# Output projection of a hybrid mixer: seven combined block products replaced by eight plain ones

## The chip, the cores and the metric

One core of a Trainium2 chip runs the whole kernel in one launch. The metric is the device time of one execution in microseconds (us). Engines are named as the profile names them: PE (TensorE, matmuls), DVE (VectorE), ACT (ScalarE), POOL (GpSimd), SP (SyncE, which here only issues DMAs). All values are float32; a matmul operand is cut into a high part and a low part, and a product of two operands is three matmuls (high by high, high by low, low by high).

## The reference

One decoder layer on 1024 tokens of width 1024. Only the first of its three residual steps is touched:

```
y_a = chunk_spatial_gating(gu, gv, ...)              # (1024 tokens, 512)
o   = gated_delta_rule(q, k, v, g, beta)             # state goes from chunk to chunk
y_b = rmsnorm(o, dn_onorm) * silu(gate)              # (1024 tokens, 512)
x   = x + concatenate([y_a, y_b], axis=-1) @ w_out   # the output projection
x   = x + CrossAttn(RMSNorm(x), RMSNorm(mem))        # memory cross-attention
x   = x + W2 relu(W1 RMSNorm(x))^2                   # the MLP, then a final RMSNorm
```

Activations are kept transposed: channels on the 128 partitions, tokens along the free dimension. `hf` is the half of the tokens (0: first 512, 1: second 512). `y_a` does not depend on the delta rule; `y_b` of a token half is known when the delta rule has passed its four chunks of 128 tokens.

## The kernel before, in words

**Order.** Input projection and the mixer's preparation come first, to about 373 us. Then a loop over 8 chunks of 128 tokens runs the delta rule. Each chunk has four steps (`chunk`, L1281 to L1330: the products with the state, with the inverse, with keys and with queries), and beside them four steps that invert the next chunk's 128x128 block (`inverse`, L1208 to L1241). The steps are short and each waits for the one before, so pieces of other work are put between them on PE: the generator `fill` hands out units of work, and `run_fill(n)` adds n to an account and runs one unit for every whole number in it. After each of the 70 places in the loop (4 steps of the first inversion, 8 x 4 chunk steps, 7 x 4 inversion steps, 6 calls between chunks) the account gets `FILL` = 0.43; 9 units run ahead of the loop (2 + 2 + `FILL0` = 5).

**The units.** 32 units prepare the cross-attention's keys and values from `mem` (each with 24 matmuls of 256 columns or 12 of 512). Each needs a 512 KB weight block: `load` puts it in one of four raw buffers, three blocks ahead; `split` cuts it into high (ACT, L134) and low parts (DVE, L135), two blocks ahead. The first 30 cuts rotate through three pairs of buffers, later ones through two (`wh`/`wl`, two buffers each). Then come 12 units of the output projection, each 12 matmuls of 128x128 by 128x512.

**The output projection before.** With the weight matrix and the activations in 2 x 2 blocks of 512, it is done by seven block products on sums and differences of blocks instead of eight plain ones. One block product is 4 units of 12 matmuls. Three of the seven are fill units: `out_use` with the first half of `y_a`, `out_use` with the difference of its halves (weights: sum of two blocks, formed on POOL), and `yb_use` with the first half of `y_b`. `out_use` adds its PSUM result to two tiles (L1079) and stores both in DRAM (`xA_d`). The other four products need the delta rule's second token half and stand after the loop, with everything for them: sums of activation blocks on DVE and POOL (`part`, L1359 to L1364), their cuts (L135), sums of weight blocks on POOL (`w_load`, `comb`, L424) and their cuts (`two`), and the evictions (L1458, L1467, L1478, L1487). `finish(c)` (L1337, L1340) transposes and gates a chunk's output; it cuts it at once only for the first token half.

**After the projection.** `x_done` stores the new x tile in DRAM, scales it for the attention (ACT, L952) and adds its square to a running sum (L205 to L209). `g_load` reads the attention's key products. The attention's first product (`split4`, `block_product`) begins at once.

**Who sets the order.** Inside `tc.manual_schedule(engines={PE})` matmuls run in the order written; the order of DVE, ACT, POOL and of SP's DMAs is set by the framework's planner on its own estimates. Before, that region ends with the last fill unit, ahead of the four late products. All engines run their queue in that fixed order.

Of the kernel before, what the change touches and what calls it, by code (L numbers as in the profile page):

```python
# [31 lines left out]
FILL0, FILL = 5, 0.43  # L32
# [203 lines left out]
def hybrid(ctx, tc, t, out):  # L236
# [720 lines left out]
    def fill():  # L957
# [79 lines left out]
        def ya_split(gi, hf):  # L1037

            a = YA[gi][hf]
            if hf == 1:  # L1040
                nc.gpsimd.tensor_tensor(a, a, YA[gi][0], op=ALU.subtract)
            hi = T(f"A{2 * gi + hf}", [P, 512], F32R)
            lo = T(f"A{8 + 2 * gi + hf}", [P, 512], F32R)
            e.split_copy(hi, lo, a)
            YX[gi][hf] = (hi, lo)

        x_in = deque()
        x_next = iter([(False, hf, p) for q in range(2) for hf in range(2) for p in (2 * q, 2 * q + 1)]
                      + [(True, 0, 0), (True, 0, 2)])

        def x_load():

            for sums, hf, p in x_next:
                if sums:
                    a = e.R("Z4 Z5", [P, 2, 512])
                    src = xA_d[p * P:(p + 2) * P, h512(hf)].rearrange("(b r) t -> r b t", r=P)
                else:
                    a = e.R("Y4 Y5 Y6 Y7", [P, 2, 512])
                    src = t["xT"][:, h512(hf)].rearrange("(b p r) t -> p r b t", b=2, r=P)[p]
                nc.sync.dma_start(a, src)  # L1060
                x_in.extend((a[:, b], p + b if sums else 4 * b + p, hf) for b in range(2))
                break

        def rows_of(w, p):
            return [v[:, :, (p % 2) * P:(p % 2) * P + P] for v in w]

        chain = {}

        def out_use(w, p, hf):

            if hf == 0:
                chain[p] = e.mm()
            ps = chain[p]
            wh, wl = rows_of(w, p)
            for k in range(4):
                e.mm3(ps[:], wh[:, k], wl[:, k], *YX[k][hf], hf == 0 and k == 0, k == 3, more=hf == 1)
            for b in range(2):
                a, m, _ = x_in.popleft()
                nc.vector.tensor_tensor(a, ps[:], a, op=ALU.add)  # L1079
                nc.scalar.dma_start(blk(xA_d, m, hf), a)  # L1080
            x_load()

        def yb_use(w, p):

            ps = e.mm()
            wh, wl = rows_of(w, p)
            for k in range(4):
                e.mm3(ps[:], wh[:, k], wl[:, k], YH[k // 2][:, k % 2], YL[k // 2][:, k % 2],
                      k == 0, k == 3)
            a, m, hf = x_in.popleft()  # L1090
            nc.vector.tensor_tensor(a, ps[:], a, op=ALU.add)
            x_done(m, hf, a, "xr0 xr1")
            x_load()
# [10 lines left out]
        ya[first_out + 1] = [(gi, 1) for gi in range(4)]  # L1104
        wo = t["w_out"]
        for q in range(2):
            for hf, src in enumerate((wo[0, q], (wo[0, 2 + q], wo[1, 2 + q]))):
                for p in (2 * q, 2 * q + 1):
                    add(src if p % 2 == 0 else None, [P, 4, 256],
                        lambda w, p=p, hf=hf: out_use(w, p, hf))  # L1110
        for q in range(2):
            for p in (2 * q, 2 * q + 1):
                add(wo[1, q] if p % 2 == 0 else None, [P, 4, 256], lambda w, p=p: yb_use(w, p))
# [5 lines left out]
        def load():  # L1119
            if need:  # L1120
                src, shape, _ = work[need.pop(0)]
                parts = []
                for d in src if isinstance(src, tuple) else (src,):
                    n = e.ring.get("raws", 0)
                    e.ring["raws"] = n + 1
                    tag = RAWS[n % len(RAWS)]
                    parts.append(T(tag, shape, F32, RAW if tag == "raw" else 1))
                    nc.sync.dma_start(parts[-1], d)
                if len(parts) == 2:
                    nc.gpsimd.tensor_tensor(parts[0], parts[0], parts[1], op=ALU.add)  # L1130
                raws_.append((parts[0], shape))
# [29 lines left out]

    fills = fill()
    debt = [0.0]

    def run_fill(n):
        debt[0] += n
        while debt[0] >= 1:
            debt[0] -= 1
            if next(fills, 1) == 1:
                debt[0] = -1e9  # L1170
# [163 lines left out]
    def finish(c, hf, sl, o, gc):  # L1334
# [3 lines left out]
        for a in range(2):  # L1338
            y = YR[hf][a][:, :, sl]
            nc.vector.tensor_tensor(y, ps[:, 256 * a:256 * a + 256].rearrange("p (h t) -> p h t", t=P),  # L1340
                                    gc[:, 2 * a:2 * a + 2], op=ALU.mult)
            if hf == 0:
                e.split_copy(YH[a][:, :, sl], YL[a][:, :, sl], y)

    def slot4(*tags):
        return [(t_[:, 0], t_[:, 1]) for t_ in (T(n, [P, 2, 512], F32R) for n in tags)]

    def split_part(q, src, sl):
        for (hi, lo), x in zip(ops_[q], src):
            e.split_copy(hi[:, sl], lo[:, sl], x[:, sl])  # L1350

    def part(sl):

        if "B22" not in ops_:
            ops_["B22"] = slot4("Z0", "Z1", "Z2", "Z3")
            ops_["T2"] = slot4("Y4", "Y5", "Y6", "Y7")
        split_part("B22", B22, sl)
        for x, y in zip(T1, B22):
            nc.vector.tensor_tensor(x[:, sl], y[:, sl], x[:, sl], op=ALU.subtract)  # L1359
        split_part("T2", T1, sl)  # L1360
        for x, y in zip(T1, B11):
            nc.gpsimd.tensor_tensor(y[:, sl], x[:, sl], y[:, sl], op=ALU.subtract)
        for x, y in zip(T1, B21):
            nc.gpsimd.tensor_tensor(y[:, sl], y[:, sl], x[:, sl], op=ALU.subtract)  # L1364


    def w_load(p):

        q, sl = p // 2, slice((p % 2) * P, (p % 2) * P + P)
        slots = ((0, 1, 2, 3, 4), (5, 7, 8, 10, 13))[p % 2]  # L1370
        a11, a12, a21, a22, s1 = (T(f"B{b}", [P, 4, P]) for b in slots)
        for a, (kb, cb) in ((a21, (0, 2 + q)), (a22, (1, 2 + q)), (a11, (0, q)), (a12, (1, q))):
            nc.sync.dma_start(a, t["w_out"][kb, cb, :, :, sl])
        comb([s1], [a21], [a22], ALU.add)
        comb([a21], [a11], [a21])
        comb([a11], [s1], [a11])
        comb([a12], [a12], [a11])
        return a12, a11, a21, a22

    def two(a, b):  # L1380

        w = [T(t_, [P, KT, P], F32R, 2) for t_ in ("wh", "wl")]
        for i, src in enumerate((a, b)):
            e.split_copy(w[0][:, 4 * i:4 * i + 4], w[1][:, 4 * i:4 * i + 4], src)
        return w
# [16 lines left out]
    YR = [[T(f"E{2 * hf + a}", [P, 2, 512]) for a in range(2)] for hf in range(2)]  # L1402
    YH, YL = ([T(f"E{4 + 2 * b + a}", [P, 2, 512], F32R) for a in range(2)] for b in range(2))
    B21, B22 = (both_halves(y) for y in YR)
    ops_ = {}
    steps(inverse(0))
    for c in range(NC):
        extra = [inverse(c + 1)] if c + 1 < NC else []
        if c == NC - 1:
            raw = w_load(0)  # L1410
# [7 lines left out]
    B11, T1 = ([y[hf] for y in YA] for hf in range(2))  # L1418
    run_fill(FILL)
    part(slice(0, 384))  # L1420
    run_fill(2)
    OUT[NC - 1]()
    part(slice(384, 512))
    run_fill(1e6)
    wa = two(*raw[:2])
    region.__exit__(None, None, None)

# [10 lines left out]
    g_load(0, 0)  # L1438

    def out_product(ps, w, b, q, start):  # L1440
        for k in range(4):
            e.mm3(ps[:], w[0][:, 4 * b + k], w[1][:, 4 * b + k], *ops_[q][k], start and k == 0, k == 3,
                  more=not start)

    def x_part(m, hf):

        a = e.R("xr0 xr1 F0 F1", [P, 512])
        nc.sync.dma_start(a, blk(xA_d, m, hf))
        return a

    for p in range(4):
        s3, a22 = raw[2:]
        a = x_part(p, 1)

        def s4_product():
            ps = e.mm()
            out_product(ps, wa, 0, "B22", True)
            nc.vector.tensor_tensor(a, ps[:], a, op=ALU.add)  # L1458

        if p == 0:  # L1460
            s4_product()
            wb = two(s3, a22)
        if p < 3:
            raw = w_load(p + 1)
        ps = e.mm()
        out_product(ps, wa, 1, "T2", True)
        nc.vector.tensor_tensor(a, ps[:], a, op=ALU.add)  # L1467
        if p > 0:
            s4_product()
        if p < 3:  # L1470
            wa = two(*raw[:2])
        if p == 0:
            ops_["T3"] = slot4("E4", "E5", "E6", "E7")
            split_part("T3", B11, slice(0, 512))
        x_done(p, 1, a, "F2 F3", nc.vector)
        a = x_part(4 + p, 1)
        out_product(ps, wb, 0, "T3", False)
        nc.vector.tensor_tensor(a, ps[:], a, op=ALU.add)  # L1478
        if p == 0:
            ops_["T4"] = slot4("Z4", "Z5", "Z6", "Z7")  # L1480
            split_part("T4", B21, slice(0, 512))
# [697 lines left out]
```

## Time and profile before

| | |
|---|---|
| median of 3 runs | 1471.27 us (1466.73 to 1472.91) |
| the profiled execution | 1479.01 us, its span 1477.3 us |
| PE busy | 1372.3 us (93% of the span), 6790 matmuls |
| DVE busy | 1196.2 us (81%) |
| ACT, POOL busy | 711.2 us (48%), 419.0 us (28%) |
| mean granted PE clock | 0.958 of full |

Busy shares are means over the whole span. Matmuls are pipelined, and their shown durations overlap: how fast they go is read from the distance of their starts. A wait is shown as idle time in front of an instruction, with the instruction that ended it.

### The profile page before, as it was taken

The page shows a single profiled execution, that of the slowest core. Times are in us where ns is not written, and L with a number is a line of the kernel's source. Part 1 is how long each engine was busy: PE and PEld are TensorE (multiplying, and loading weights), DVE is VectorE, ACT ScalarE, POOL GpSimd, SP SyncE. Part 2 cuts the span into 40 slices and gives each one's busy share as a digit, 9 for nine tenths or more (in the row PEclk, how much of TensorE's full clock was granted, in tenths as well). Part 3 has the DMA queues.
Part 4 walks back from the last instruction along what each step waited for, and adds up shares of the span by engine and source line. Part 5 has one row for each costly group of instructions (what it writes and reads, how often), then busy time and mean ns, then how long its engine had stood idle before and what let it go on. Part 6 is the DMA issues. An engine that isn't in the chain of part 4 may idle for free.

```text
span 1477.3 us, 19249 instructions
## 1 busy us (share of the span) xinstructions
PE 1372.3 (93%) x6790; PEld 1134.7 (77%) x6790; DVE 1196.2 (81%) x1795; ACT 711.2 (48%) x1266; POOL 419.0 (28%) x314
## 2 busy tenths in 40 slices
PE   9989989889999988889979799999998999999996
PEld 8767777668898766667758588888886788888885
DVE  8798878798577788899999976776777998787775
ACT  7453565646455436565746644344443443333432
POOL 7542545520311263773495600000000000000024
PEclk9999999989999998999989899999999999999996
DMA  5103344539988865414000144444446754534203
GB/s 202 44 29 100 101 136 118 146 119 342 298 270 249 270 235 156 158 63 149 17 29 1 43 157 150 157 157 157 156 139 232 280 186 154 171 128 143 71 1 114
DMA packets 144979, 215.27 MB, mean 146 GB/s; under 512 B 22897, under 2 KB 82289, under 8 KB 144882
## 3 DMA queue, kind: packets, MB, share of 16 engines
q1 hardware_dynamic: 92320, 156.79, 33.6%
q10 hardware_dynamic: 52562, 57.25, 11.3%
q8 instruction: 53, 0.87, 0.2%
q14 instruction: 44, 0.36, 0.1%
HBM read 145.84 MB, written 68.16 MB: 145 GB/s over the span
## 4 chain that ended last, share of the span: by engine, by line
PE 48%; DVE 20%; DMA 5%; issue 4%; ACT 3%; POOL 1%; ACTq 0%; DVEq 0%; SPq 0%; POOLq 0%
PE mm L155 10%; PE mm L156 10%; PE mm L157 9%; PE dn L155 5%; PE dn L156 5%; PE dn L157 5%; DVE Z L135 3%; DVE Y L135 3%; DVE wl L135 2%; DVE F L607 1%; DVE A L1726 1%; DVE rw L2059 1%; DMA hid_T_d<-F 1%; DMA g_d<-A 1%; ACT wh L134 1%
## 5 line engine op out<-in xcount | busy, mean ns | idle before, releaser
L2041 POOL TENSOR_TENSOR rB<-rB,fq 128x256 f32<-128x256 f32 (+1 forms) x18 | 18.9, 1050 | 596.4 <-ACT fq L2039 595.9
L155 PE MATMUL mm<-A,wh 128*128 128x512 f32 (+1 forms) x336 | 124.7, 371 | 7.8 <-ACT F L518 5.3
L157 PE MATMUL mm<-A,wl 128*128 128x512 f32 (+1 forms) x336 | 122.9, 366 | 0.0
L134 ACT CAST wh<-raw 128x512 fp32r<-128x512 f32 (+1 forms) x105 | 78.9, 767 | 71.9 <-PE dn L156 22.8
L135 DVE TENSOR_TENSOR wl<-raw,wh 128x512 fp32r<-128x512 f32 (+1 forms) x99 | 94.9, 960 | 16.7 <-ACT wh L134 16.3
L156 PE MATMUL mm<-B,wh 128*128 128x512 f32 x220 | 89.6, 407 | 0.0
L134 ACT CAST sp<-rw 128x1024 fp32r<-128x1024 f32 x36 | 37.6, 1051 | 92.5 <-issue 42.0
L155 PEld LDWEIGHTS mm<-A,wh 128*128 128x128 f32 x336 | 66.7, 199 | 18.0 <-ACT F L518 6.1
L157 PEld LDWEIGHTS mm<-A,wl 128*128 128x128 f32 x336 | 66.8, 199 | 9.2 <-DVE wl L135 0.5
L155 PE MATMUL mm<-Z,wh 128*128 128x512 f32 x130 | 53.1, 410 | 7.8 <-DVE xr L1478 4.2
L155 PE MATMUL mm<-sp,sp 128*128 128x512 f32 (+1 forms) x152 | 58.1, 385 | 2.1 <-DVE A L2085 2.1
L156 PE MATMUL mm<-sp,sp 128*128 128x512 f32 (+1 forms) x152 | 58.2, 383 | 1.6 <-DVE sp L135 1.6
L424 POOL TENSOR_TENSOR B<-B,B 128x512 f32<-128x512 f32 x32 | 47.6, 1503 | 41.6 <-DMA B<-in_w_out_dram 18.9
L157 PE MATMUL mm<-sp,sp 128*128 128x512 f32 (+1 forms) x152 | 58.1, 383 | 0.0
L1922 DVE TENSOR_TENSOR F<-raw 128x512 f32<-128x512 f32 x15 | 10.4, 691 | 58.0 <-DMA raw<-in_ffn_w_dram 58.0
L156 PE MATMUL mm<-Z,Z 128*128 128x512 f32 (+1 forms) x136 | 53.6, 394 | 2.8 <-DVE Z L135 2.7
L135 DVE TENSOR_TENSOR sp<-rw,sp 128x1024 fp32r<-128x1024 f32 x36 | 43.8, 1218 | 14.3 <-ACT sp L134 14.3
L156 PE MATMUL mm<-Z,wh 128*128 128x512 f32 x130 | 53.1, 408 | 0.3 <-DVE Z L135 0.3
L155 PE MATMUL mm<-Z,Z 128*128 128x512 f32 (+1 forms) x136 | 53.4, 393 | 0.0
L157 PE MATMUL mm<-Z,wl 128*128 128x512 f32 x130 | 53.1, 409 | 0.0
L157 PE MATMUL mm<-Z,Z 128*128 128x512 f32 (+1 forms) x136 | 53.0, 390 | 0.0
L2017 DVE TENSOR_TENSOR A<-mm,A 128x512 f32<-128x512 f32 x64 | 43.5, 685 | 9.6 <-PE mm L157 9.4
(702 smaller groups left out, 4629.4 us busy)
## 6 DMA issues: line engine op xcount, KB each, us to landing
raw<-in_ffn_w_dram SPq DMA_DIRECT2D x32, 512.0 KB, 3.7
raw<-in_w_in_dram SPq DMA_DIRECT2D x20, 512.0 KB, 3.9
rw<-hid_T_d SPq DMA_DIRECT2D x18, 512.0 KB, 3.3
hid_T_d<-F ACTq DMA_DIRECT2D x33, 256.0 KB, 2.4
rw<-hid_B_d SPq DMA_DIRECT2D x14, 512.0 KB, 3.3
Z<-in_ffn_w_dram SPq DMA_DIRECT2D x12, 512.0 KB, 4.4
rw<-in_ffn_w_dram SPq DMA_DIRECT2D x12, 512.0 KB, 4.8
hid_B_d<-F ACTq DMA_DIRECT2D x22, 256.0 KB, 2.4
```

The costliest lines, as they stand in the source:

```text
L134: nc.scalar.copy(hi, src)
L135: (lo_eng or nc.vector).tensor_tensor(lo, src, hi.bitcast(F32), op=ALU.subtract)
L155: nc.tensor.matmul(out, wh, xh, start=start, stop=False, skip_group_check=more)
L156: nc.tensor.matmul(out, wh, xl, start=False, stop=False, skip_group_check=more)
L157: nc.tensor.matmul(out, wl, xh, start=False, stop=stop, skip_group_check=more)
L424: eng.tensor_tensor(x, y, z_, op=op)
L607: nc.vector.scalar_tensor_tensor(acc, pre[:, tap:tap + 512], g_of("conv", 12 * tap + self.blk), acc, op0=ALU.mult, op1=ALU.add)
L1726: nc.vector.tensor_tensor(acc, ps[:], acc, op=ALU.add)
L1922: nc.vector.tensor_tensor(s1, a21, a22, op=ALU.add)
L2017: nc.vector.tensor_tensor(acc, ps[:], acc, op=ALU.add)
L2041: nc.gpsimd.tensor_tensor(self.sa, self.sa, self.sq, op=ALU.add)
L2059: nc.vector.scalar_tensor_tensor(ob[:, b], acc, g_of("norm_final", m), rb, op0=ALU.mult, op1=ALU.mult)
```

## The change

The output projection becomes eight plain block products, 32 units of 12 matmuls: 16 with `y_a` (both halves), 8 with the first half of `y_b`, 8 with its second half. All are units of `fill`, which has 64 units instead of 44. `FILL` goes from 0.43 to 0.56. Units 57 to 64 (second half of `y_b`) are held back until a last call; units 49 to 56 are called behind the loop, two ahead of the last `finish` and six behind it. `finish` cuts both halves of `y_b`. `part`, `w_load`, `two`, the weight sums and the whole section of four late products go. The region in which PE's order is the written one now reaches to the last unit. The attention's `g_load`s stand ahead of the last 8 units.

```
-FILL0, FILL = 5, 0.43
+FILL0, FILL = 5, 0.56
...
-            if hf == 1:
-                nc.gpsimd.tensor_tensor(a, a, YA[gi][0], op=ALU.subtract)
...
+        x_next = iter([(False, hf, c) for c in range(4) for hf in range(2)]
+                      + [(True, hf, c) for hf in range(2) for c in range(4)])
...
+        def out_use(w, b, ops_):
+            ps = e.mm()
+            wh, wl = (v[:, :, b * P:(b + 1) * P] for v in w)
             for k in range(4):
+                e.mm3(ps[:], wh[:, k], wl[:, k], *ops_(k), k == 0, k == 3)
             a, m, hf = x_in.popleft()
             nc.vector.tensor_tensor(a, ps[:], a, op=ALU.add)
+            if b == 1:
+                x_load()
+            return a, m, hf
+
+        def ya_use(w, b, hf):
+            a, m, hf = out_use(w, b, lambda k: YX[k][hf])
+            nc.scalar.dma_start(blk(xA_d, m, hf), a)
+
+        def yb_use(w, b, hf):
+            a, m, hf = out_use(w, b, lambda k: tuple(v[hf][k // 2][:, k % 2] for v in (YH, YL)))
+            x_done(m, hf, a, ("xr0 xr1", "F2 F3")[hf], (None, nc.vector)[hf])
...
+        for c in range(4):
+            for hf in range(2):
+                for b in range(2):
+                    add(wo[0, c] if hf + b == 0 else None, [P, 4, 256],
+                        lambda w, b=b, hf=hf: ya_use(w, b, hf))
+        for hf in range(2):
+            if hf == 1:
+                before.append(len(work))
+            for c in range(4):
+                for b in range(2):
+                    add(wo[1, c] if b == 0 else None, [P, 4, 256],
+                        lambda w, b=b, hf=hf: yb_use(w, b, hf))
...
+    def run_fill(n, last=False):
         debt[0] += n
+        while debt[0] >= 1 and (last or not before or ran[0] < before[0]):
             debt[0] -= 1
+            ran[0] += 1
...
         for a in range(2):
-            y = YR[hf][a][:, :, sl]
+            y = e.R("B2 B3", [P, 2, P])
             nc.vector.tensor_tensor(y, ps[:, 256 * a:256 * a + 256].rearrange("p (h t) -> p h t", t=P),
                                     gc[:, 2 * a:2 * a + 2], op=ALU.mult)
-            if hf == 0:
-                e.split_copy(YH[a][:, :, sl], YL[a][:, :, sl], y)
+            e.split_copy(YH[hf][a][:, :, sl], YL[hf][a][:, :, sl], y)
...
-    run_fill(FILL)
-    part(slice(0, 384))
     run_fill(2)
     OUT[NC - 1]()
-    part(slice(384, 512))
-    run_fill(1e6)
-    wa = two(*raw[:2])
-    region.__exit__(None, None, None)
+    run_fill(60)
...
+    for hp in range(2):
+        for kb in range(2):
+            g_load(kb, hp)
+    debt[0] = 0.0
+    run_fill(1e6, True)
+    region.__exit__(None, None, None)
```

## Rows read from the trace of the kernel before

**Rows 1.** Windows: length, busy of PE, PEld, DVE, ACT, POOL, PEclk, DMA share, GB/s.
```profile
373.40:531.10 157.70, 151.65 (x1265) 136.06 (x1265) 108.61 (x213) 73.74 (x129) 43.47 (x35) 0.96 0.89 275
531.10:622.10 91.00, 73.38 (x280) 56.21 (x279) 81.10 (x103) 46.89 (x91) 49.84 (x40) 0.89 0.51 169
622.10:660.00 37.90, 32.21 (x151) 26.30 (x150) 37.43 (x49) 22.12 (x46) 29.75 (x19) 1.00 0.16 55
373.40:499.60 126.20, 122.11 (x1060) 110.87 (x1060) 83.79 (x164) 64.06 (x112) 30.30 (x25) 0.95 0.88 270
499.60:531.10 31.50, 29.54 (x207) 25.19 (x205) 24.82 (x50) 9.68 (x18) 13.16 (x10) 1.00 0.91 298
```

**Rows 2.** Timeline of PE: start us, length us, instruction; [idle before it <-releaser].
```profile
530.27 1.06 PE L1314 MATMUL dn<-B,Z 128*128 128x128 f32 x8
531.09 0.48 PE L155 MATMUL mm<-A,wh 128*128 128x512 f32 x1
...
621.69 0.55 PE L157 MATMUL mm<-Z,wl 128*128 128x512 f32 x1
```

**Rows 3.** Timeline of PE, first and last matmul of one fill unit.
```profile
543.22 0.39 PE L155 MATMUL mm<-E,wh 128*128 128x512 f32 x1
...
545.71 0.39 PE L157 MATMUL mm<-E,wl 128*128 128x512 f32 x1
```

**Rows 4.** Waits of PE from 531.1 to 622.1 us: total us, times, longest.
```profile
PE mm L155 <- DVE Y L1079: 5.6, 1, 5.6
PE mm L155 <- DVE xr L1478: 4.2, 1, 4.2
PE mm L155 <- DVE F L1478: 3.6, 1, 3.6
PE mm L155 <- ACT wh L134: 2.9, 2, 1.9
PE mm L157 <- DVE wl L135: 1.0, 1, 1.0
PE mm L156 <- DVE Z L135: 0.3, 1, 0.3
```

**Rows 5.** Timeline of DVE around the longest of these waits.
```profile
547.35 3.08 DVE L135 TENSOR_TENSOR Y<-Y,Y 128x384 fp32r<-128x384 f32 x3
550.34 1.27 DVE L1079 TENSOR_TENSOR Y<-mm,Y 128x512 f32<-128x512 f32 x2
```

**Rows 6.** Timeline of PE inside the loop, at 485 to 489 us.
```profile
488.38 0.63 PE L155 MATMUL mm<-wh,A 128*128 128x512 f32 x1
488.80 0.63 PE L156 MATMUL mm<-wl,A 128*128 128x512 f32 x1
```

**Rows 7.** Waits of PE from 373 to 531.1 us, the two longest in total.
```profile
PE dn L1218 <- DVE X L1212: 2.7, 2, 2.3
PE dn L1289 <- DVE B L1283: 1.6, 1, 1.6
```

**Rows 8.** Groups of DVE from 531 to 622 us, by form: busy us, mean ns | idle before.
```profile
L135 DVE TENSOR_TENSOR wl<-Z,wh 128x1024 fp32r<-128x1024 f32 x2 | 3.7, 1838 | 0.0
L1079 DVE TENSOR_TENSOR Y<-mm,Y 128x512 f32<-128x512 f32 x4 | 2.6, 681 | 1.0 <-PE mm L157 1.0
L1340 DVE TENSOR_TENSOR E<-dn,B 128x256 f32<-128x256 f32 x4 | 1.5, 410 | 0.0
```

**Rows 9.** Timeline of POOL, the scaling of chunk 7's output.
```profile
538.56 1.35 POOL L1330 TENSOR_TENSOR F<-F,of 128x512 f32<-128x512 f32 x1
```

**Rows 10.** DMA of 373.4 to 499.6 us, and the x stores of 500 to 620 us.
```profile
DMA packets 32154, 34.04 MB, mean 270 GB/s; under 512 B 8587, under 2 KB 24374, under 8 KB 32141
...
x_d<-xr ACTq DMA_DIRECT2D x6, 256.0 KB, 2.5
```

**Rows 11.** Groups of ACT from 531 to 622 us, by form: casts to the high part.
```profile
L134 ACT CAST Z<-E 128x512 fp32r<-128x512 f32 x4 | 2.3, 614 | 0.0
L134 ACT CAST wh<-Z 128x1024 fp32r<-128x1024 f32 x1 | 1.1, 1055 | 0.1
```

More of the change, by code (lines that the diff above doesn't have):

```diff
@@ L1047, in fill @@
         x_in = deque()
-        x_next = iter([(False, hf, p) for q in range(2) for hf in range(2) for p in (2 * q, 2 * q + 1)]
-                      + [(True, 0, 0), (True, 0, 2)])
+        x_next = iter([(False, hf, c) for c in range(4) for hf in range(2)]
+                      + [(True, hf, c) for hf in range(2) for c in range(4)])
         def x_load():
[L1053 to L1061, printed above, removed]
-                break
@@ L1064, in rows_of @@
[L1064 to L1069, printed above, removed]
-            if hf == 0:
-                chain[p] = e.mm()
-            ps = chain[p]
-            wh, wl = rows_of(w, p)
-            for k in range(4):
[L1076 to L1089, printed above, removed]
+            for sums, hf, c in x_next:
+                a = e.R("Y4 Y5 Y6 Y7", [P, 2, 512])
+                src = (xA_d if sums else t["xT"])[2 * c * P:(2 * c + 2) * P, h512(hf)]
+                nc.sync.dma_start(a, src.rearrange("(b r) t -> r b t", r=P))
+                x_in.extend((a[:, b], 2 * c + b, hf) for b in range(2))
+                break
@@ L1090, in yb_use @@
+        def out_use(w, b, ops_):
+            ps = e.mm()
+            wh, wl = (v[:, :, b * P:(b + 1) * P] for v in w)
+            for k in range(4):
+                e.mm3(ps[:], wh[:, k], wl[:, k], *ops_(k), k == 0, k == 3)
             a, m, hf = x_in.popleft()
             nc.vector.tensor_tensor(a, ps[:], a, op=ALU.add)
-            x_done(m, hf, a, "xr0 xr1")
-            x_load()
+            if b == 1:
[4 more added lines that the diff above has]
+            nc.scalar.dma_start(blk(xA_d, m, hf), a)
@@ L1103, in fill @@
         ya = {first_out - 4 + gi: [(gi, 0)] for gi in range(4)}
-        ya[first_out + 1] = [(gi, 1) for gi in range(4)]
+        for gi in range(4):
+            ya.setdefault(first_out + gi // 2, []).append((gi, 1))
         wo = t["w_out"]
[L1106 to L1113, printed above, removed]
+        for c in range(4):
[10 more added lines that the diff above has]
+                        lambda w, b=b, hf=hf: yb_use(w, b, hf))
         need = [n for n, (src, _, _) in enumerate(work) if src is not None]
@@ L1121, in load @@
                 src, shape, _ = work[need.pop(0)]
[L1122 to L1131, printed above, removed]
+                n = e.ring.get("raws", 0)
+                e.ring["raws"] = n + 1
+                tag = RAWS[n % len(RAWS)]
+                raws_.append((T(tag, shape, F32, RAW if tag == "raw" else 1), shape))
+                nc.sync.dma_start(raws_[-1][0], src)
         def split():
@@ L1160, in fill @@
             yield
+    before = []
     fills = fill()
     debt = [0.0]
-    def run_fill(n):
+    ran = [0]
+    def run_fill(n, last=False):
         debt[0] += n
-        while debt[0] >= 1:
+        while debt[0] >= 1 and (last or not before or ran[0] < before[0]):
             debt[0] -= 1
+            ran[0] += 1
             if next(fills, 1) == 1:
@@ L1338, in finish @@
         for a in range(2):
-            y = YR[hf][a][:, :, sl]
+            y = e.R("B2 B3", [P, 2, P])
             nc.vector.tensor_tensor(y, ps[:, 256 * a:256 * a + 256].rearrange("p (h t) -> p h t", t=P),
                                     gc[:, 2 * a:2 * a + 2], op=ALU.mult)
-            if hf == 0:
-                e.split_copy(YH[a][:, :, sl], YL[a][:, :, sl], y)
[L1345 to L1385, printed above, removed]
+            e.split_copy(YH[hf][a][:, :, sl], YL[hf][a][:, :, sl], y)
     for n in INV:
@@ L1400, in hybrid @@
     run_fill(FILL0)
[L1402 to L1405, printed above, removed]
+    YH, YL = ([[T(f"E{4 - 4 * hf + 2 * b + a}", [P, 2, 512], F32R) for a in range(2)]
+               for hf in range(2)] for b in range(2))
     steps(inverse(0))
@@ L1408, in hybrid @@
         extra = [inverse(c + 1)] if c + 1 < NC else []
-        if c == NC - 1:
-            raw = w_load(0)
         steps(chunk(c), *extra)
@@ L1417, in hybrid @@
                 run_fill(FILL)
-    B11, T1 = ([y[hf] for y in YA] for hf in range(2))
-    run_fill(FILL)
-    part(slice(0, 384))
     run_fill(2)
     OUT[NC - 1]()
-    part(slice(384, 512))
-    run_fill(1e6)
-    wa = two(*raw[:2])
-    region.__exit__(None, None, None)
+    run_fill(60)
     GB = [[[None] * 4 for _ in range(2)] for _ in range(2)]
@@ L1436, in g_load @@
             GB[kb][hp][k] = a
[L1438 to L1481, printed above, removed]
-        x_done(4 + p, 1, a, "F2 F3", nc.vector)
-        a = x_part(4 + p, 0)
-        out_product(ps, wb, 1, "T4", False)
-        if p < 3:
-            wb = two(*raw[2:])
-        nc.vector.tensor_tensor(a, ps[:], a, op=ALU.add)
-        x_done(4 + p, 0, a, "F2 F3", nc.vector)
-        if p == 2:
-            g_load(1, 0)
-    g_load(0, 1)
-    g_load(1, 1)
+    for hp in range(2):
[4 more added lines that the diff above has]
+    region.__exit__(None, None, None)
     sc1 = T("sc1", [P, NC])
```

## The prediction

> **What bounds the kernel now.** The busy shares of the whole span say only that PE leads, so I cut the span into the stages that the change touches. The windows by stage come first [rows 1]. The reader is to compare PE and DVE there. In the loop (373.4 to 531.1 us, 157.7 us) PE is busy for 151.7 us and DVE for 108.6; in the tail behind it (531.1 to 622.1 us, 91.0 us) PE is busy for 73.4 only and DVE for 81.1. So PE binds the loop, and DVE's queue binds the tail.
>
> The borders are in PE's timeline [rows 2]: the loop is cut from the first inversion's first matmul on, the last product of chunk 7 is followed by a fill unit at 531.09, and the last late product ends at 622.1. One unit of 12 matmuls of 512 columns has 11 starts in 545.71 - 543.22 = 2.49 us [rows 3], 0.226 us each; a unit is 12 x 0.226 = 2.72 us. The 0.39 us beside each row is the pipelined length and prices nothing.
>
> The tail holds 6 fill units (the account stands at 9 + 70 x 0.43 = 39.1 at the end of the loop, and the 39th runs behind the last product, so 38 of 44 are done) and 4 products of 4 units: 22 units, 59.8 us, and two transposes of `finish`, 0.9 us. 91.0 - 59.8 - 0.9 = 30.3 us are lost. The waits of PE show 17.6 us of it, of which 5.6, 4.2 and 3.6 us end with an eviction by DVE [rows 4]. DVE's timeline shows why for the longest: the eviction at 550.34 stands behind three cuts of `y_a` sums and starts the moment the last of them ends [rows 5]. The rest is the clock: PEclk is 0.89 in the tail [rows 1], a mean over its two levels (2.4 GHz, and 1.2 GHz as where matmuls start 0.42 us apart [rows 6]): 2 x 0.11 x 91 = 20 us ran at the lower, which costs 10 us.
>
> **The change part by part.** The profiled execution took 1479.0 us (span 1477.3); the sum is made against it and then moved to the median, 1471.3, which is 7.7 us lower.
>
> *Loop, added.* 9 + 70 x 0.56 = 48.2: 48 units by the end of the loop, 47 of them ahead of 531.09's counterpart, instead of 38. PE is idle for 157.7 - 151.7 = 6.0 us there [rows 1], so there is no room to hide in: 9 x 2.72 = **+24.5 us**.
>
> *Loop, removed.* The longest waits are 2.7 and 1.6 [rows 7]; the clock (0.96) costs 2 x 0.04 x 157.7 / 2 = 6.3. With a unit behind every 1.8 steps instead of every 2.3, fewer steps wait for DVE without a unit between them. I take **-2.5 us**; bounds +14 (DMA, below) and -7.4 (both waits gone, 4.3, and half of the clock's loss, 3.1).
>
> *Loop, at no cost.* Each `ya_use` unit has one eviction and one store where `out_use` had two, and one weight block per four units. `finish` now cuts `y_b` also for chunks 4 to 7: per chunk two cuts of 128x256, some 0.41 us each on DVE by the gating row of that size [rows 8], and two casts on ACT. DVE's idle 49 us in the loop cover it; without cover 4 x 0.8 = 3.3 us. The POOL subtraction of `y_a` halves goes and saves nothing: POOL is idle for 114 of 158 us.
>
> *Tail.* Out go 22 units, the sums, the cuts and the evictions of the late products; in come 1 + 2 + 6 + 8 = 17 units: 46.2 us, and 0.9 for `finish`. DVE then has 17 evictions of 0.68, 8 cuts of a 128x1024 block at up to 1.84 [rows 8], 8 square sums, and the end of chunk 7: some 37 us of 50, where it had 81 of 91. What late stalls remain is bounded by 0 and by the tail's rate of before, 30.3 / 22 = 1.38 us per unit, 23.4 us. The nearest row is the stretch 499.6 to 531.1, where output units already run beside the delta rule with DVE busy for 24.8 of 31.5 us, PE idle for 2.0 and the clock at 1.00 [rows 1]. That gives 3 us for 47; with one half-speed spell of 6 us (3 us) I take **6 us**. The last `finish` is covered: three units (8.2 us) and a transpose stand ahead of it, and chunk 7's chain took 8.6 us from its last product's end (531.3) to the end of POOL's scaling at 539.9 [rows 2, 9], with DVE full of cuts. So the tail goes from 91.0 to 46.2 + 0.9 + 6 = 53.1: **-37.9 us**.
>
> *The DMAs.* `g_load` (16 of 256 KB) now stands ahead of the last units on SP's queue. Behind it come only the last x tile pair, which is needed 6 units (16 us) later, and the last gating tile that it may wait for is free after the last `finish`. x pairs are fetched three pairs (6 units) ahead. All cost 0, at most one late pair, 3 us, inside the bounds of the stalls.
>
> *A wait added.* The attention's first product cuts its fourth key tile into Y7, which holds the last x pair until that is stored: eviction 0.68, store 2.5 [rows 10], cast 0.61 [rows 11], cut 0.68 make 4.5 us, and nine matmuls (2.0 us) can go ahead. Behind the cast stand ACT's next casts, and PE waits for them. **+2 us**; bounds 0 (another order) and 4.5. In DVE's load at 622 to 660 us, 37.4 of 37.9, nothing is gained: the tail before already held most of these cuts.
>
> Sum: 24.5 - 2.5 - 37.9 + 2 = **-13.9 us**: 1465.1 on the profiled basis, **1457.4** on the median's.
>
> **The rivals.**
>
> *DMA keeps the loop's first part at its pace.* Until the 32 units with `mem` are done (to 499.6 us), a unit comes after 1.79 steps instead of 2.33, so 23 units take 41.1 steps instead of 53.5. A step costs (157.7 - 29 x 2.72) / 70 = 1.13 us, so this part should shrink by 14 us. Its 34.04 MB [rows 10] would then need 303 GB/s instead of 270, and a DMA share of 0.99 instead of 0.88. If that is not to be had, the 14 us come back: -13.9 + 14.0 = 0, 1471.4. For: the share. Against: two blocks cut and three loaded ahead, no wait of PE for a weight, and windows up to 298 GB/s at 0.91 [rows 1]. Chance 0.14. The Trainium skill (Perfetto Trace Analysis, Identifying the Most-Contended Engine and Engine Utilization) would not judge DMA by such a share but by its bytes against 358 GB/s; by that 303 fits, and this rival would fall.
>
> *The tail stalls at its old rate*, because the planner again puts cuts ahead of evictions: 23.4 instead of 6, +3.5 us, 1474.8. Against: the work that stood ahead of them is gone. Chance 0.07.
>
> *Slower: the two weight buffers.* Every cut from the 31st on uses two pairs of `wh`/`wl` only, so the cast of the block after next waits until PE has left its buffer. If each of the 12 weight blocks then stops PE for cast and cut, 1.05 + 1.84 = 2.9 us [rows 8, 11], that is 34.7 us in place of the 6: +14.8, 1486.1. It decides from (13.9 + 6 + 7.4) / 12 = 2.3 us per block. Against: a block lasts two units (5.4 us) or four (10.9), and PE waited little for casts where output units ran before (2.9 us in all of the tail [rows 4]). Chance 0.10.
>
> *PE has room in the loop.* The weight loads (PEld) are busy for 136.1 of 157.7 us [rows 1]; were the other 21.6 free, the nine units would cost 2.9 instead of 24.5: -35.5, 1435.8. Against: units start matmuls 0.226 us apart without a gap. Chance 0.04. This is how the Trainium skill would read it: Perfetto Trace Analysis, Identifying the Most-Contended Engine, takes the busy share of weight loads and not that of matmuls as the measure of PE's headroom.
>
> *All stalls go* (loop -7.4, tail 0, attention 0): 24.5 - 7.4 - 43.9 = -26.8, 1444.5. Chance 0.08.
>
> **How the numbers follow.** The forecast has 0.57, its own range 1450 to 1465. A measurement of this kernel can tell about 0.5%, 7.4 us: faster is below 1463.9, slower above 1478.6. Faster: 0.55 of the forecast's 0.57, 0.08 and 0.04, 0.67. No change: the rest of the forecast, DMA and the old rate, 0.23. Slower: 0.10. For 8 in 10 the range takes in the forecast, all stalls gone and both cases of no change: 1443 to 1475.
>
> **What would show it.** Right: the last product of chunk 7 some 180 us behind the first inversion (157.7 before) with PE idle under 8 us in all; from there to the end of the last unit about 53 us with PEclk above 0.95; POOL busy for less than half of its 49.8 us before; a wait of 2 to 3 us for a cast or cut in the attention's first product. Wrong: PE waiting for weight casts or for DMA in the loop, DVE evictions behind other cuts in the tail, or a loop that grows by much less than 22 us.

## The result, and the profile after

The changed kernel takes 1453.59 us (median of 4 runs, 1452.05 to 1458.79) where the kernel before, run beside it, takes 1472.09 (4 runs, 1466.73 to 1475.56): 18.5 us less. The ratio on record, which is not the quotient of these two medians, is 0.9884 [0.9845, 0.9923], some 17 us. The forecast was 1457.4. The profiled execution took 1453.84 us, its span 1452.1, its mean granted clock 0.970.

The windows of the kernel after come first: loop, tail, attention's start, and the loop's part in which units with `mem` run (columns: length, busy of PE, PEld, DVE, ACT, POOL, PEclk, DMA share, GB/s).

```profile
371.50:543.80 172.30, 170.98 (x1372) 152.29 (x1373) 108.84 (x222) 76.65 (x137) 26.05 (x22) 0.99 0.86 271
543.80:591.10 47.30, 47.30 (x215) 39.18 (x214) 35.38 (x49) 32.40 (x55) 17.82 (x12) 1.00 0.65 219
591.10:629.00 37.90, 30.68 (x129) 23.94 (x127) 33.18 (x38) 17.39 (x35) 32.40 (x22) 0.91 0.12 42
371.50:484.50 113.00, 111.68 (x968) 101.86 (x969) 74.26 (x145) 62.33 (x105) 21.62 (x18) 0.98 0.93 291
```

Beside [rows 1] the reader is to see three things. The loop is longer, 172.3 us for 157.7, and PE is idle in it for 1.3 us instead of 6.0. The tail is half as long, 47.3 for 91.0, PE is idle for nothing of it, its clock is 1.00 instead of 0.89, and DVE is busy for 35 of 47 us instead of 81 of 91. And attention's start, which had a clock of 1.00 and PE busy for 32.2 of 37.9 us, now has 0.91 and 30.7: something was given back there.

| part | before | after | difference | predicted |
|---|---|---|---|---|
| start to the loop | 373.4 | 371.5 | -1.9 | 0 |
| loop | 157.7 | 172.3 | +14.6 | +22.0 |
| tail | 91.0 | 47.3 | -43.7 | -37.9 |
| attention to the end | 855.2 | 861.0 | +5.8 | +2 |
| sum | 1477.3 | 1452.1 | -25.2 | -13.9 |

These are two single executions, and that of before was a long one, 6.9 us over its median (1479.0 against 1472.1); that is the 6.7 us by which this sum passes 18.5.

PE's waits in the loop of after, and then from its end to 640 us (total us, times, longest), against [rows 7] and [rows 4]:

```profile
PE dn L1194 <- DMA Tc<-ti_d: 1.6, 1, 1.6
PE dn L1225 <- ACT B L1215: 0.9, 1, 0.9
PE dn L1204 <- DVE X L1198: 0.4, 1, 0.4
...
PE mm L156 <- DVE Y L135: 3.6, 2, 2.8
PE dn L155 <- DVE wh L1479: 2.0, 1, 2.0
PE dn L155 <- ACT rs_t L171: 1.5, 1, 1.5
PE dn L1436 <- DVE wh L1479: 1.0, 1, 1.0
PE mm L155 <- ACT Y L134: 0.7, 1, 0.7
```

The 1.6 us of the first line lie in front of the loop's first matmul. None of the waits is for a weight's cast or cut in the loop or the tail, and the first of the second list stands in attention's first product. PE's timeline shows it there:

```profile
592.24 0.39 PE L157 MATMUL mm<-Y,Y 128*128 128x512 f32 x1
593.37 0.73 PE L155 MATMUL mm<-Y,Y 128*128 128x512 f32 x2 [0.74 <-ACT Y L134]
...
597.36 0.80 PE L156 MATMUL mm<-Y,Y 128*128 128x512 f32 x1 [2.79 <-DVE Y L135]
597.95 0.63 PE L157 MATMUL mm<-Y,Y 128*128 128x512 f32 x1
598.38 0.63 PE L155 MATMUL mm<-Y,Y 128*128 128x512 f32 x1
...
604.10 0.50 PE L156 MATMUL mm<-Y,Y 128*128 128x512 f32 x1 [0.85 <-DVE Y L135]
```

Six matmuls run, ACT's half of a key tile is late, four later DVE's half, and after the 2.79 us the matmuls start 0.43 us apart (597.95 to 598.38), the lower clock, until 602.6. The waits are 4.4 us, and 12 starts at 0.43 instead of 0.226 another 2.4. DVE's timeline at that place, then POOL's:

```profile
592.18 1.77 DVE L135 TENSOR_TENSOR Z<-A,Z 128x512 fp32r<-128x512 f32 x1
593.87 0.68 DVE L1064 TENSOR_TENSOR Y<-mm,Y 128x512 f32<-128x512 f32 x1
594.47 1.16 DVE L209 TENSOR_TENSOR rB<-rB,F 128x512 f32<-128x512 f32 x1
595.55 1.75 DVE L135 TENSOR_TENSOR Y<-B,Y 128x512 fp32r<-128x512 f32 x1
```

```profile
591.67 3.41 POOL L424 TENSOR_TENSOR B<-B,B 128x512 f32<-128x512 f32 x2
595.04 1.71 POOL L424 TENSOR_TENSOR E<-A,A 128x512 f32<-128x512 f32 x1
```

The last unit's result was ready at 591.3 (its last matmul starts at 590.88), but its eviction (593.87) stands behind a cut of 1.77 us, and the cut that PE waits for (595.55) behind eviction and square sum. POOL adds blocks for the attention (L424) at this time, one addition after the other. In these lines only DVE's operations on two tiles of SBUF are long beside them (a cut 1.75 to 1.77 us, a square sum 1.16, for 0.68): the eviction, which reads one operand from PSUM, keeps its 0.68 us at 593.87.

### The profile page after: what moved, and what is told of

Read it like the earlier page. It is cut to its first block, busy times and chain, and to the rows that moved or that the text cites. A ratio compares the mean times of both kernels' runs of the same rounds, so it can differ in the third digit from the quotient of the medians.

```text
span 1452.1 us, 19205 instructions
## 1 busy us (share of the span) xinstructions
PE 1366.1 (94%) x6838; PEld 1131.9 (78%) x6838; DVE 1152.2 (79%) x1753; ACT 702.0 (48%) x1240; POOL 379.1 (26%) x280
## 5 line engine op out<-in xcount | busy, mean ns | idle before, releaser
L155 PE MATMUL mm<-A,wh 128*128 128x512 f32 (+1 forms) x368 | 138.5, 376 | 6.9 <-ACT F L518 4.4
L157 PE MATMUL mm<-A,wl 128*128 128x512 f32 (+1 forms) x368 | 135.1, 367 | 0.0
L134 ACT CAST wh<-raw 128x512 fp32r<-128x512 f32 (+1 forms) x108 | 82.0, 775 | 73.6 <-PE mm L156 22.9
L135 DVE TENSOR_TENSOR wl<-raw,wh 128x512 fp32r<-128x512 f32 (+1 forms) x102 | 99.3, 975 | 20.6 <-ACT wh L134 20.2
L155 PEld LDWEIGHTS mm<-A,wh 128*128 128x128 f32 x368 | 72.5, 197 | 18.5 <-ACT F L518 5.1
L157 PEld LDWEIGHTS mm<-A,wl 128*128 128x128 f32 x368 | 72.5, 197 | 10.7 <-DVE wl L135 0.5
L156 PE MATMUL mm<-A,wh 128*128 128x256 f32 (+1 forms) x192 | 61.9, 322 | 0.0
L135 DVE TENSOR_TENSOR sp<-rw,sp 128x1024 fp32r<-128x1024 f32 x36 | 43.7, 1217 | 14.6 <-ACT sp L134 14.6
L155 PE MATMUL mm<-Z,Z 128*128 128x512 f32 (+1 forms) x136 | 53.1, 390 | 0.0
L156 PEld LDWEIGHTS mm<-B,wh 128*128 128x128 f32 x220 | 43.9, 200 | 8.9
L1774 ACT ACTIVATE F<-F 128x512 f32<-128x512 f32 x31 | 19.6, 633 | 52.3 <-DVE F L1773 52.3
L1902 DVE TENSOR_TENSOR A<-dn,A 128x512 f32<-128x512 f32 x48 | 32.7, 685 | 13.7 <-PE dn L157 13.1
```

Of the source, the lines that this page charges most:

```text
L134: nc.scalar.copy(hi, src)
L135: (lo_eng or nc.vector).tensor_tensor(lo, src, hi.bitcast(F32), op=ALU.subtract)
L155: nc.tensor.matmul(out, wh, xh, start=start, stop=False, skip_group_check=more)
L156: nc.tensor.matmul(out, wh, xl, start=False, stop=False, skip_group_check=more)
L157: nc.tensor.matmul(out, wl, xh, start=False, stop=stop, skip_group_check=more)
L1774: nc.scalar.activation(o, o, AF.Square)
```

## The experiments

Each kernel ran beside the kernel before on the same chip; ratios are to it, with a 95% interval.

**1. Is DVE's queue the bound of the tail of before?** The low cuts of the late products' activations go.

```
-        return [(t_[:, 0], t_[:, 1]) for t_ in (T(n, [P, 2, 512], F32R) for n in tags)]
+        return [(t_[:, 0], t_[:, 0]) for t_ in (T(n, [P, 2, 512], F32R) for n in tags)]
...
-            e.split_copy(hi[:, sl], lo[:, sl], x[:, sl])
+            nc.scalar.copy(hi[:, sl], x[:, sl])
```

> The kernel before, with the low parts of the four late products' activation operands left out: their 16 cuts (and the partial ones) on DVE go, and the high part stands in for the low part, so PE does the same 192 late matmuls. This leaves out part of the computation. Theory (the tail is bound by DVE's queue): DVE loses about 23 us of its 81 us in the tail, and the time falls by 8 to 18 us, with PE's waits for evictions L1079 and L1478 mostly gone. Rival (the tail is bound by PE, its clock or the DMAs): within 3 us of before.

Measured: 1458.51 us, 0.9906 [0.9877, 0.9936], 14.2 us less than before (1472.66). Its tail:

```profile
523.70:602.30 78.60, 67.99 (x279) 53.79 (x278) 65.50 (x79) 47.24 (x91) 48.99 (x40) 0.91 0.62 201
```

PE has the same matmuls as in [rows 1] (280 and 279 records); DVE has 15.6 us less to do, and the tail is 12.4 us shorter. So DVE's work set at least this much of the tail's length. Of the waits that were expected to go, that for L1079 is gone and one for L1478 is still 3.5 us; a wait of 5.2 us for a cast on ACT is new.

**2. How much of it is POOL's?** POOL's sums of the late weight blocks go, all of DVE's work stays.

```
-        comb([s1], [a21], [a22], ALU.add)
-        comb([a21], [a11], [a21])
-        comb([a11], [s1], [a11])
-        comb([a12], [a12], [a11])
```

> The kernel before without POOL's sums of the late products' weight blocks (this part of the computation is left out), all else as it was, DVE's cuts too. Theory: the tail of before is bound by the amount of DVE's work; POOL's sums only stretch it a little, and the time moves by less than 3 us. Rival: DVE is the bound of the tail only because its cuts take longer while POOL's sums run; then the cuts shorten, the tail loses 5 us or more, and the time falls by 3 to 10 us.

Measured: 1464.01 us, 0.9955 [0.9935, 0.9976], 6.9 us less than before (1470.93). The rival's band was met, and its reason is seen in the groups of DVE from the loop's end to attention's first product, first of before, then without the sums (mean ns behind the comma):

```profile
L135 DVE TENSOR_TENSOR wl<-B,wh 128x512 fp32r<-128x512 f32 x16 | 14.0, 915 | 3.9 <-ACT wh L134 3.9
L135 DVE TENSOR_TENSOR Z<-E,Z 128x512 fp32r<-128x512 f32 x4 | 5.7, 1494 | 0.0
L135 DVE TENSOR_TENSOR E<-Y,E 128x512 fp32r<-128x512 f32 x4 | 3.8, 959 | 0.0
```

```profile
L135 DVE TENSOR_TENSOR wl<-B,wh 128x512 fp32r<-128x512 f32 x16 | 11.9, 780 | 1.6 <-ACT wh L134 1.6
L135 DVE TENSOR_TENSOR E<-Y,E 128x512 fp32r<-128x512 f32 x4 | 2.6, 682 | 0.0
L135 DVE TENSOR_TENSOR Z<-E,Z 128x512 fp32r<-128x512 f32 x4 | 2.5, 686 | 0.0
```

The same cuts of 128x512 take 0.69 us instead of 0.96 and 1.49. So theory and rival each have a part: the amount of DVE's work binds (experiment 1), and POOL's sums lengthen it by some 7 us. From the loop's end to a fixed point of the attention (the wait of PE for `rs_t` that ends at 654.9 in before) DVE is busy for 106.6 of 114.2 us here and for 113.7 of 123.8 in before, so it stays the fullest engine.

**3. The one lost stretch of before's loop.** At 483 to 492 us before loses a wait of 2.33 us for DVE [rows 7] and a spell of lower clock behind it [rows 6], while POOL adds two weight blocks for the difference product. Those sums go:

```
-                if len(parts) == 2:
-                    nc.gpsimd.tensor_tensor(parts[0], parts[0], parts[1], op=ALU.add)
```

> The kernel before, with the POOL additions of two weight blocks (L1130, two of 128x1024) left out, all transfers kept; so the product with the difference of the y_a halves uses one block only, part of the computation is left out. Theory (the loop's wait of 2.3 us at 486 us and the half-speed spell behind it come from DVE cuts slowed by this POOL addition): the wait is gone, the loop is 5 to 6 us shorter. Rival (the wait comes from the turn of the units itself, or from DMA): the wait stays and the time is within 2 us of before.

Measured: 1470.99 us, 0.9988 [0.997, 1.0006]; its profiled loop is 153.9 us, without that wait. By the median the sums cost under 2 us, which fits the prediction's sentence that POOL's work in the loop saves nothing when it goes. But the profiled loops differ: 157.7 in before and 157.1 in experiment 2 (sums kept, wait and spell at the same place), 151.9 in experiment 1 (sums kept, neither), 153.9 here. The first two executions were 6.9 and 5.5 us above their kernels' medians, the last two within 1 us of theirs. The traces show what differs. DVE has the same order here in all four: two cuts of 128x256 stand ahead of the copy (L1212) that PE waits for. In before POOL's sum runs at the same time as these cuts; in experiment 1 it starts after them (DVE, then POOL, of before and then of experiment 1):

```profile
482.78 2.89 DVE L135 TENSOR_TENSOR E<-E,E 128x256 fp32r<-128x256 f32 x2
482.95 2.44 POOL L1130 TENSOR_TENSOR raw<-raw,Z 128x1024 f32<-128x1024 f32 x1 [1.18 <-DMA Z<-in_w_out_dram]
```

```profile
480.50 0.74 DVE L135 TENSOR_TENSOR E<-E,E 128x256 fp32r<-128x256 f32 x2
481.70 2.39 POOL L1130 TENSOR_TENSOR raw<-raw,Z 128x1024 f32<-128x1024 f32 x1 [2.20 <-DMA Z<-in_w_out_dram]
```

In experiment 2 the two meet (2.89 us for the cuts), in experiment 3 there is no sum (0.75 us). So theory and rival each have a part again: the wait comes from POOL's sum, but only where the sum, which starts when a transfer has landed, falls on these two cuts. The loop without this event has about 152 to 154 us. How often it comes is not known from four profiles.

**4. Is the gain the filling rate alone?** The kernel before with the new rate: `FILL0, FILL = 5, 0.56`.

> The kernel before with FILL 0.56, so all 44 units run inside the loop. Theory (a unit costs its 2.7 us wherever PE is dense; what the change won was the late stalls): five units more in the loop, +13.6 us, and six fewer behind it; the late sums and cuts still bind the tail, which shrinks by less than these units: -6 to +6 us in all. Rival (the denser filling of the loop is the source of the gain): faster by 10 us or more.

Measured: 1478.96 us, 1.0051 [1.0025, 1.0077], slower by half a per cent (6.3 us by the medians, some 7.5 by the ratio), a little past the theory's band of 6; the rival (faster) falls. PE's waits say where it goes:

```profile
PE mm L155 <- ACT Z L134: 7.6, 1, 7.6
PE dn L1314 <- ACT B L1290: 7.2, 1, 7.2
PE dn L1337 <- POOL F L1330: 5.4, 1, 5.4
```

The 44 units are used up before the loop ends, and the last chunk's steps (L1314), the last `finish` (L1337) and the first late product wait uncovered, 20.2 us in all. The rate needs the 20 new units.

**5. And the new units without the rate?** The kernel after with `FILL0, FILL = 5, 0.43`.

> The changed kernel with the old FILL of 0.43: nine units move from the loop to behind it. Theory (PE is dense in both stages, a unit costs 2.7 us in either): within 4 us of the changed kernel; the loop back to about 150 us, the tail at about 72. Rival (filling between steps hides units in time that PE would lose): slower by 5 to 20 us, since the steps lose their cover.

Measured: 1460.85 us, 0.9932 [0.9903, 0.9961], 5.4 us more than the kernel after beside it (1455.41, 0.9899 [0.9866, 0.9932]), past the theory's 4 and at the low end of the rival's band. Its loop is 152.4 us and its tail of 26 units 71.8. Against the loop of 172.3, 9 units more cost 19.9 us and not 24.5: each saves half a microsecond. PE's idle time in the loop goes from 4.2 to 1.3 us and its clock from 0.98 to 0.99, which is most of these 4.6 us. The kernel after itself, run again, kept loop and tail to 0.1 us (172.3, 47.3):

> The changed kernel again, as the measure for the three runs beside it: 0.985 to 0.992 of the kernel before.

**6. More units in the loop.** The kernel after with 0.72, and later with 0.66.

> The changed kernel with FILL 0.72: units 49 to 56 move from behind the loop into it, and the 23 units with mem come in 32 steps instead of 41. Theory (PE binds both stages): within 4 us of the changed kernel, the loop 8 units (22 us) longer and the tail as much shorter. Rival (the DMAs bind the loop's first part at some rate): that part would need about 340 GB/s for 34 MB in about 100 us; if 300 is the limit, PE waits there and the time is 8 to 15 us above the changed kernel.

> The kernel after with a filling rate of 0.66 instead of 0.56 units a step: some 55 units in the loop, not used up before its end, and so about one left for the tail among those that don't wait. Theory: the loss of a_fill72 came from units that were used up before the last chunk's chain, which then stood uncovered; with units to the last step the time is within 4 us of the kernel after, 0.985 to 0.992 of the kernel before. Rival: more units per step cost more than they save in the tail, by DMA or by steps held up; then it is some 5 us slower than the kernel after and the loop grows by more than 2.72 us for each unit added.

Measured: 1465.00 us, 0.9941 [0.9917, 0.9966] with 0.72, and 1465.74, 0.9964 [0.994, 0.9987] with 0.66. By the ratios that is 6 to 8 and 10 to 12 us more than the kernel after (0.9884 and 0.9899 in its two comparisons). With 0.72 the first part of the loop moves its data at 298 GB/s and PE is idle for 0.9 of 105.2 us; then its longest wait up to 640 us:

```profile
374.80:480.00 105.20, 104.33 (x872) 94.95 (x873) 67.67 (x123) 58.38 (x95) 17.43 (x14) 0.98 0.95 298
```

```profile
PE dn L1323 <- POOL F L1316: 4.6, 1, 4.6
```

Most of its loss is behind the loop: the tail has 31.0 us for 8 units, the transposes and 3 matmuls of the attention (23.3), since no unit is left to cover the last chunk's chain (L1323 is its transpose); the loop grows by 28.1 us for 9 units (24.5). With 0.66 the tail has 37.0 us for 10 units, the transposes and some matmuls of the attention (about 30), with waits of 2.0 and 2.1 us, and the loop grows by 27.5 us for 7 units (19.0). So my theory, which had only the chain's cover, falls, and the rival (more than 2.72 us for each unit added: 3.9) holds. PE and then ACT at that place:

```profile
482.14 1.11 PE L1225 MATMUL dn<-B,B 64*64 64x64 f32 x8 [4.85 <-ACT B L1215]
```

```profile
469.65 3.21 ACTq L1023 DMA_DIRECT2D vw_d<-A  x2
472.96 0.59 ACT L1021 COPY A<-mm 128x512 f32<-128x512 f32 x1 [3.77 <-DMA B<-vt_d]
...
477.80 3.66 ACTq L1023 DMA_DIRECT2D vw_d<-A  x4
481.50 0.59 ACT L1215 COPY B<-dn 128x512 f32<-128x512 f32 x1 [3.25 <-DMA vw_d<-A]
```

ACT, which also issues the stores of the prepared values (`vw_d`), is idle twice, for 3.77 and 3.25 us, while it issues such stores: 3.21 us for two and 3.66 for four, where two take 0.9 to 1.7 us in the kernel after between 445 and 481 us. The profile puts the ends of these waits down to a load (`vt_d`) and a store (`vw_d`); the copy that a step of the inversion needs stands behind, PE waits 4.85 us, and two slices of 3.4 us at a clock of 0.50 and 0.56 follow (3.2 lost): 8.1 of the 8.5 us that the loop has too much. So the DMA rival shows in a form that I did not think of, through ACT's queue and not through a late weight; that full DMA queues made these issues long is argued, not shown. It is one execution, 4.3 us above its kernel's median (1470.0 against 1465.7), and with 0.72 it does not show; how often it comes stays open.

**7. The wait at attention's start.** The last four x pairs take other buffers, so that the attention's key tiles find Y4 to Y7 free.

```
-                a = e.R("Y4 Y5 Y6 Y7", [P, 2, 512])
+                a = e.R("Z0 Z1 Z2 Z3" if sums and hf else "Y4 Y5 Y6 Y7", [P, 2, 512])
```

> The changed kernel, with the last four x pairs loaded into Z0 to Z3 instead of Y4 to Y7, so that the attention's first product can cut its key tiles into Y4 to Y7 without waiting for the last x store. Theory (this wait, 4.4 us of PE idle in all, and the half-speed spell behind it, 3.4 us, are what made the attention start 5.8 us later than predicted from nothing): 4 to 8 us faster than the changed kernel, PE idle at the attention's start under 1.5 us. Rival (the cuts are late because DVE is full, at 1.77 us a cut beside POOL's sums): the waits stay, within 2 us.

Measured: 1450.04 us, 0.9856 [0.9824, 0.9889], 5.4 us less than the kernel after. Attention's first product has no wait from its first matmul (592.64) to its last (603.30):

```profile
592.64 0.39 PE L155 MATMUL mm<-Y,Y 128*128 128x512 f32 x1
...
603.30 0.39 PE L157 MATMUL mm<-Y,Y 128*128 128x512 f32 x1
603.52 0.39 PE L155 MATMUL dn<-Z,Z 128*128 128x512 f32 x1
```

A fixed point behind it tells the gain apart from the rest of the kernel, whose length differs by some us between executions. From the end of the last unit to the end of PE's wait for `rs_t` it is 32.8 us in before, 40.6 in the kernel after (both its profiles) and 36.3 here: 4.3 us are given back, 3.5 are not. DVE is busy for 36.1 of these 36.3 us, so the rival (DVE is full) has that part.

Run once more on another chip, it gave 1450.60 us, 0.9868 [0.9838, 0.9897], and again 36.3 us to that point. The kernel after did not run beside it there:

> The kernel a_xtiles once more, as the reference for a_xhalf on the same chip. Theory: 0.983 to 0.989 of the kernel before, attention's first product without a wait. Rival: the gain of a_xtiles over the kernel after was chance, and the ratio is 0.989 to 0.993.

**8. Does PE bind to the end of the tail?** Each of the last 8 units runs over half of the inner dimension, 48 matmuls (10.9 us) fewer; first in the kernel after, then with the buffers of experiment 7.

```
-            for k in range(4):
-                e.mm3(ps[:], wh[:, k], wl[:, k], *ops_(k), k == 0, k == 3)
+            for k in ks:
+                e.mm3(ps[:], wh[:, k], wl[:, k], *ops_(k), k == 0, k == ks[-1])
...
-            a, m, hf = out_use(w, b, lambda k: tuple(v[hf][k // 2][:, k % 2] for v in (YH, YL)))
+            a, m, hf = out_use(w, b, lambda k: tuple(v[hf][k // 2][:, k % 2] for v in (YH, YL)),
+                              range(2) if hf else range(4))
```

> The changed kernel, where the last eight units use only two of four blocks of the inner dimension: 48 matmuls fewer, everything else kept (part of the computation is left out). 48 is just the number by which eight plain products exceed seven. Theory (PE binds the tail): 48 x 0.226 = 10.9 us faster, if the evictions and the attention's start keep up, 6 to 11 us. Rival (another engine or the DMAs bind the tail): under 3 us.

> The kernel after with two edits together: the last four pairs of activations take the tiles Z0 to Z3 (as in a_xtiles), and each of the last eight units runs over half of the inner dimension (as in a_half; this part of the computation is left out). Theory: the 48 matmuls saved in a_half (10.9 us) were given back because the casts that attention's first product needs waited for the tiles of the units; with other tiles that wait is gone, and the time lies 6 to 10 us below a_xtiles, 0.979 to 0.982 of the kernel before. Rival: what holds the casts is DVE's square sums at attention's start, slowed beside POOL's weight sums, and the ACT buffers behind them; the tiles then matter little, and the time is less than 4 us below a_xtiles, with a wait of PE for ACT's or DVE's halves of 5 us and more in attention's first product.

Measured: 1453.42 us, 0.9885 [0.9851, 0.9918], 2 us less than the kernel after; and with the other buffers 1455.58, 0.9899 [0.9871, 0.9927], 5 us more than experiment 7 beside it. Both theories fall. PE and DVE in the second of them:

```profile
588.78 0.79 PE L155 MATMUL mm<-Y,Y 128*128 128x512 f32 x1 [5.34 <-ACT Y L134]
592.65 0.79 PE L156 MATMUL mm<-Y,Y 128*128 128x512 f32 x1 [3.08 <-DVE Y L135]
```

```profile
582.42 0.68 DVE L1064 TENSOR_TENSOR Z<-mm,Z 128x512 f32<-128x512 f32 x1
583.02 1.18 DVE L209 TENSOR_TENSOR rB<-rB,F 128x512 f32<-128x512 f32 x1
584.12 0.68 DVE L1064 TENSOR_TENSOR Z<-mm,Z 128x512 f32<-128x512 f32 x1
584.72 6.19 DVE L209 TENSOR_TENSOR rB<-rB,F 128x512 f32<-128x512 f32 x4
590.84 6.81 DVE L135 TENSOR_TENSOR Y<-B,Y 128x512 fp32r<-128x512 f32 x4
```

PE reaches this place some 9 us earlier (38.7 us of tail for 47.3) and waits: DVE works almost without a gap, and four square sums of 1.5 us each stand ahead of the first cut of a key tile. The buffers bring no gain here, as the rival said. From the end of the last unit to the end of the wait for `rs_t` DVE is busy for 45.5 of 46.0 us in both halved kernels. From chunk 7's last product on, this point comes after 84.7 us in both, after 87.9 in the kernel after and after 83.6 in experiment 7. So most or all of the 10.9 us that PE is spared comes back as waits for these casts and cuts. DVE's order differs too: in the second run of experiment 7 the four cuts come between the square sums (at 570.80, 576.84, 583.08 and 585.60), so whether DVE's amount or the planner's order costs more in the two halved kernels is not told apart. Of the 5 us by which the second one is behind experiment 7, the profiles show 1.1 up to that point; the rest stays open.

## Why the prediction was right, and where its terms were off

The direction and the time came out (1457.4 forecast, 1453.6 measured, own range 1450 to 1465), and both halves of the mechanism are shown: the tail of before was bound by DVE (experiments 1 and 2), and the loop pays for the moved units (experiment 5). With the loop of experiment 5, which has the same number of units as before, in place of the long one of before, the terms are: loop some +20 (172.3 against 152.4), tail -43.7, attention +5.8, together -18 for the measured -18.5. The forecast had +22.0, -37.9 and +2. That the sum came within 4 us is in part luck: the tail was forecast 5.8 us and the loop 2 us too long, the attention 3.8 us too short.

*Loop, added and removed.* 24.5 us of units went in as counted. What they removed is 4.6 us (experiment 5: 24.5 - 19.9) and not 2.5, inside the bounds given. The profiled pair says 9.9 (24.5 - 14.6), by which the prediction's own sign of being wrong, a loop that grows by much less than 22 us, would have been met; the rest fits the event of experiment 3 in the profiled execution of before. The base was a long execution, and the prediction moved its sum to the median without asking which term the 7.7 us sat in; by the loops of experiments 1, 3 and 5 (151.9 to 153.9 us for 157.7) some 4 to 6 us of them sat in the loop.

*Loop, at no cost.* The added cuts and casts of `finish` are hidden: PE is idle for 1.3 us in the loop of after. That POOL's work there saves nothing holds by the median (experiment 3); in an execution where a sum falls on DVE's two cuts it does cost.

*Tail.* This is the term most off: 53.1 predicted, 47.3 measured. Units and transposes are 47.1 us, as counted; the late stalls are 0.2 instead of 6. They were sized by the stretch 499.6 to 531.1 [rows 1], but 1.6 of PE's 2.0 us of idle time there are a wait of a step of the delta rule (L1289 [rows 7], at 525.5), and the tail has no such steps. The half-speed spell did not come. Once the cuts and POOL's sums had gone, no eviction came late and the clock held at 1.00. The last `finish` was covered, as said; experiment 6 shows the price when it is not.

*DMAs.* 0, as priced, with this rate.

*A wait added.* The place and the cause were right, the size was not: +2 predicted, with a bound of 4.5, against +7.8 to the wait for `rs_t` (40.6 for 32.8 us; behind it the profile of after is 2.0 us shorter, which makes the +5.8 of the table). Experiment 7 gives 4.3 of it back there, 5.4 by the medians. Two things lengthen the chain. The eviction and the cut wait in DVE's queue, where beside POOL's sums a cut takes 1.77 us and not the 0.68 that I used; and the lower clock after the wait costs a further 2.4 us, which the bound left out. The 3.5 us that stay without the wait are DVE's: it is busy for 36.1 us to that point where it had 32.6 in before, so the cuts that the tail of before already held do count, against the prediction's sentence on them.

*The rivals.* DMA keeping the loop's first part at its pace: it did not. Its 32 units end some 13 us earlier (113.0 us against 126.2) at 291 GB/s and a share of 0.93, and 298 were reached in experiment 6. Old rate of stalls: none were left. Two weight buffers: no wait of PE for a cast or cut of a weight in loop or tail. All stalls gone: the tail did that, attention's start did the opposite.

PE with room in the loop: no. PEld is busy for 152.3 of 172.3 us in after, a share of 0.88, and yet 9 units cost 19.9 us (experiment 5) and not 2.9. The Trainium skill (Perfetto Trace Analysis, Identifying the Most-Contended Engine) judges PE's headroom by this share, beside the matmul work done as a share of the peak. By the share alone 12% would be left here, and the measurement decides against it.

## What to carry to other kernels

When work is moved to fill between dependent steps, count its full price in the stage that takes it, look for the gain in the stage that it leaves, and keep enough units back to cover the chain behind the last step: rates that use them up early lost 6 to 12 us here. Then look at the first consumer behind the shortened stage and at which buffers it takes over: a choice of tiles was worth 5 us more. And once PE had no stall left up to a border, fewer matmuls in front of it gained 2 us in one kernel and nothing in the other: PE then waited for DVE, which was busy for 99% of the stretch behind it.

## What the hardware showed that I had not expected

- A cut of 128x512 on DVE takes 0.68 us alone and 1.77 beside POOL's additions of the same size, while an eviction from PSUM keeps its 0.68; in the tail of before the additions cost 6.9 us by the median (experiment 2).
- Waits of 2.8 and 4.9 us on PE were followed by 5 to 7 us at the lower clock (matmuls 0.43 us apart instead of 0.226), and cost 2.4 and 3.2 us more than their length.
- With the DMAs at a share of 0.91, no weight came late, but in one execution ACT stood idle for 3.8 and 3.3 us while it issued its own stores, with a step of the delta rule behind it (experiment 6).
